# Bias rows on 128 partitions and eight strided loads, a padded weight layout, and attention one step earlier, in a one-layer hybrid of attention and mLSTM

## The chip, the cores and the metric

The kernel runs on one NeuronCore of a Trainium2 chip. A core has five engines with their own instruction streams: TensorE (PE) multiplies matrices, VectorE (DVE), ScalarE (ACT) and GpSimd (POOL) work element by element, and SyncE (SP) issues nearly all DMAs here. Each engine runs its instructions in the order in which they were issued to it, and waits on semaphores for what others produce. The time is that of one execution on the device, in microseconds (us). The profile is of one execution; spans and busy times are from it.

## What is computed

One layer for one sequence of 256 tokens with a model width of 1024. Cut to what matters:

```python
ada = c @ w_ada + b_ada                       # shift, scale, gate
h = rmsnorm(x, norm_w) * (1 + scale) + shift
qa, ka, va, za, qm, km, vm, zm, om, ig, fg, ga, gm = split(h @ w_in)
qa, ka = rmsnorm per head (8 heads of 128)
bias[h, i, j] = rel_bias[bucket(i - j), h]    # 32 buckets; -1e30 where j > i
ya = softmax(qa @ ka.T / sqrt(128) + bias) @ va     # 256 tokens are one block: plain causal attention
ya = (ya * silu(za)) @ w_att_proj
qm, km = silu(causal conv of width 4 over [qm, km])
hm = mLSTM(qm, km, vm, ig, fg)                # 4 heads of 256
ym = (rmsnorm(sigmoid(om) * hm) * silu(zm)) @ w_ml_proj
y = sigmoid(ga) * ya + sigmoid(gm) * ym
out = x + gate * (y @ w_out)
```

All arrays are float32. The bias depends on i - j alone, so a head's bias matrix is made of shifted copies of one row of 384 values: the matrix's row p is that row from place 127 - p on.

## The kernel before

Large products are made from two halves of each operand: a rounded high part (type fp32r) and the rest as a low part, and three products high x high, high x low, low x high. So every weight tile that comes in by DMA (`raw`) is cast by ACT to its high part (`wh`, L448) and then DVE (at eight places POOL) subtracts to get its low part (`wl`, L452).

**Phase 1** (`P1_STEPS`, L303 to L320) makes `hTh` and `hTl`, the modulated input, transposed, in 8 pieces of 128 rows, and at the same time the q and k products (2048 columns of `w_in`, the tensor `w_row`), piece by piece in the order in which their rows come in. A letter of `P1_STEPS` is an operation, its digit the piece. `next_loads` issues the loads of `P1_LOADS`: `A` is half a piece of `w_ada` (512 KB, contiguous), `W` a column range of a piece of `w_row` (`W_PIECES`: 128 rows of 2048 or 6144 bytes). The first row matmul (L198) needs `hTh` of piece 0 (L168) and the cast of `W00` (L183), which stand in ACT's order as `w0`, then `H0`. POOL meanwhile copies the bias table into the row `rvec` (`rel_prep`, L283 to L292). At the end of the phase SP writes it to DRAM (`rel_write`, L301), between loads of `w_va`.

**Phase 2** runs over 23 chunks of at most 512 columns (`chunks`): va in three, then za, qm, km, att, zm, vm, om, ga, gm, ml and out in two halves each. A chunk is four steps g, one for 256 of the 1024 rows that are summed. Steps 0 to 11 are va (12 matmuls of 344 columns a step), 12 to 19 za (24 matmuls of 256 columns), 20 to 35 qm and km. In each step g (loop at L948) the program issues, in this order:

- `split(g + 4)`: ACT's cast, then what `between` hangs on step g, then DVE's low split. So weights are split four steps ahead; a cast waits for its buffer until the matmuls of step g - 1 are done (five buffers).
- at the first step of a chunk, the eviction of the chunk before (`EV`). za's first half is the exception: `ev_za` stands further down, at L969.
- what `at` hangs on step g, in the order of registration
- `pump()`: the next weight loads whose buffer is free (six buffers)
- the step's matmuls

The small work hangs on steps by hand (L867 to L923). `bias_read` at step 0 reads the bias matrices `Tb` (128 rows, 8 heads, 256 columns) back from DRAM in four loads of 32 neighbouring partitions. `qk_T` transposes q and k on PE in two halves of four heads, with an eviction by ACT. Attention of head h runs from `A0`, which is 11: at step A0 + h PE makes the scores (`att_qk`), DVE adds the bias and takes the maximum (L608, L610), ACT the exponential (`att_exp`); a step later DVE normalises (`att_norm`); at A0 + 3 + h PE transposes the probabilities and ACT copies them out (`att_PT`). `att_av` multiplies two heads with va, DVE multiplies with silu(za) (`yf`, L648). `gates_0` to `gates_7`, `gates_T` and `gates_D` make the mLSTM's decay matrices; `gates_2` is a logarithm, `gates_5` and `gates_D` exponentials. ACT loads a table (ACT_TABLE_LOAD) when it changes between these, the attention's exponentials and Silu.

All of this shares four PSUM banks, `aux`, which are given out in turn: the fifth request gets the first bank again and waits until its reader is done. `qk_T` asks for two banks, `att_qk`, `att_PT`, `att_av`, `gates_0` and `gates_T` for one each.

Of the kernel before, what the change touches and what calls it, by code (L numbers as in the profile page):

```python
# [66 lines left out]
def tile_hybrid(ctx: ExitStack, tc: tile.TileContext, x, c, params2, w_row, w_va, ada_mod, ada_gate,  # L67
# [21 lines left out]
    rvec = consts.tile([AH, 384], F32, name="rvec")  # L89
# [9 lines left out]
    rvd = dram.tile([32, AH, 384], F32, name="rvd")  # L99
# [9 lines left out]
    relT = prm[0:AH, P_RT:P_RT + BUCKETS]  # L109
# [173 lines left out]
    def rel_prep(part):  # L283
        bk = rel_bucket_starts()
        one = BUCKETS // 2
        if part == 0:
            nc.gpsimd.tensor_copy(rvec[:, 256 - one:256], relT[:, one:])
        for b in range(one + 4 * part, one + 4 * part + 4):
            ds_ = [d for d in range(S) if bk[d] == b]
            m0, m1 = 255 - max(ds_), 255 - min(ds_) + 1  # L290
            r = BUCKETS - 1 - b
            nc.gpsimd.tensor_copy(rvec[:, m0:m1], relT[:, r:r + 1].to_broadcast([AH, m1 - m0]))  # L292
# [7 lines left out]
    def rel_write():  # L300
        nc.sync.dma_start(rvd.rearrange("b h m -> h b m"), rvec[:, None, :].to_broadcast([AH, 32, 384]))  # L301
# [155 lines left out]
    def at(step, fn, *a):  # L457
        hooks.setdefault(step, []).append((fn, a))
# [38 lines left out]
    def bias_read():  # L497
        L = 384
        Tb = slot("bias", [128, AH, S], F32, "Tb")
        for a in range(4):  # L500
            src = bass.AP(tensor=rvd.tensor, offset=rvd.offset + 127 - 32 * a,
                          ap=[[AH * L - 1, 32], [L, AH], [1, S]])
            nc.sync.dma_start(Tb[32 * a:32 * a + 32], src)
        T["Tb"] = Tb
# [373 lines left out]
    at(5, gates_0)  # L878
    at(6, qk_T, "q", 0)
    at(7, qk_T, "k", 0)  # L880
    at(10, qk_T, "q", 1)
    at(12, qk_T, "k", 1)
    A0 = 11
# [5 lines left out]
    for step, fn in ((6, gates_1), (9, gates_2), (11, gates_3), (13, gates_copy), (14, gates_4), (16, gates_5),  # L889
                     (18, gates_6), (18, gates_T), (19, gates_7), (22, gates_D)):  # L890
        at(step, fn)
# [6 lines left out]
    for q in range(2):  # L898
        at(done("za", 0) + 1 + q, att_av, 2 * q)
        at(done("za", 1) + 1 + q, att_av, 4 + 2 * q)  # L900
# [47 lines left out]
    for g in range(NG):  # L948
# [20 lines left out]
        if g == done("za", 0):  # L969
            ev_za(mmt[C["za", 0]], 0)  # L970
# [55 lines left out]
def _lay_out(x, c, w_ada, b_ada, norm_w, w_in, q_norm_w, k_norm_w, rel_bias, conv_w, conv_b, b_igate, b_fgate,  # L1026
# [6 lines left out]
    params[0:AH, P_RT:] = rel_bias.T[:, ::-1]  # L1033
# [9 lines left out]
    w_row = w_in[0, :, :NR].reshape(KT, 128, NR)  # L1043
# [29 lines left out]
```

## Time and profile before

| | us |
|---|---|
| median of 3 runs (352.56 to 353.26) | 352.77 |
| the profiled execution | 352.9 |
| its span, first to last instruction | 351.1 |
| busy: PE, DVE, ACT, POOL | 345.3, 247.3, 215.8, 89.0 |

The span is 1.8 us shorter than the profiled execution's own time. The granted TensorE clock is 1.000 over the span. A row of a timeline reads: start, duration, engine, line, operation, what it writes <- what it reads, sizes, count, and in brackets how long its engine had been idle before it and what ended that. SPq is SP's queue: the time of a DMA there is that of issuing it. A row of the waits reads: who waited for whom, total us, times, longest.

### The profile page before, as it was taken

Reading aid. Unit: us, or ns where it says so; the run is one execution under the profiler, and the core shown is the slowest. Engines: PE = TensorE matmul, PEld = TensorE weight load, DVE = VectorE, ACT = ScalarE, POOL = GpSimd, SP = SyncE. Lnnn points to the kernel's source line nnn. Section 1 sums busy time; section 2 is a strip of 40 time slices with the busy share of each in tenths; the row PEclk is TensorE's granted clock in tenths of the full one; section 3 lists DMA queues with packets and bytes.
Section 4 is the critical chain, followed back from the end, with each engine's and each line's share of the span. In section 5 each row is a group of like instructions: output and inputs, shape, how many; then the busy total and the mean of one; then the engine's idle time right before and its main releaser. Section 6 shows DMA issues by size and latency. Waiting matters only on the chain.

```text
span 351.1 us, 6176 instructions
## 1 busy us (share of the span) xinstructions
PE 345.3 (98%) x2432; PEld 322.7 (92%) x2432; DVE 247.3 (70%) x369; ACT 215.8 (61%) x333; POOL 89.0 (25%) x81
## 2 busy tenths in 40 slices
PE   8999999999999999999999999999999999999996
PEld 7687889999999999999998888888899999999996
DVE  6899996966976528768975593764475775469961
ACT  4768779978978696775636554545646374443510
POOL 4300002880202443554104252000010420452000
PEclk9999999999999999999999999999999999999999
DMA  7999999996571463393784836649219229382011
GB/s 265 398 414 414 418 417 328 246 257 256 212 271 59 134 227 121 126 410 125 289 311 136 343 121 239 241 148 385 67 23 357 100 53 365 124 269 91 3 62 60
DMA packets 23573, 77.99 MB, mean 222 GB/s; under 512 B 2928, under 2 KB 4984, under 8 KB 22904
## 3 DMA queue, kind: packets, MB, share of 16 engines
q1 hardware_dynamic: 23392, 77.07, 60.9%
q10 hardware_dynamic: 152, 0.53, 0.4%
q8 instruction: 19, 0.31, 0.4%
q14 instruction: 10, 0.08, 0.1%
HBM read 76.14 MB, written 1.45 MB: 221 GB/s over the span
## 4 chain that ended last, share of the span: by engine, by line
PE 82%; DVE 7%; DMA 4%; ACT 4%; issue 1%; POOL 0%; SPq 0%; POOLq 0%; ACTq 0%; DVEq 0%
PE mm L1004 13%; PE mm L1007 13%; PE mm L1006 13%; PE pm L198 12%; PE mm L997 6%; PE mm L998 6%; PE mm L999 6%; DMA raw<-in_w_in_dram 4%; PE mm L990 3%; DVE wl L452 3%; ACT wh L448 2%; PE xps L263 1%; PE mm L1017 1%; PE mm L1019 1%; PE mm L1018 1%
## 5 line engine op out<-in xcount | busy, mean ns | idle before, releaser
L452 DVE TENSOR_TENSOR wl<-raw,wh 128x1024 fp32r<-128x1024 f32 (+1 forms) x92 | 118.9, 1303 | 65.3 <-ACT wh L448 65.3
L448 ACT CAST wh<-raw 128x1024 fp32r<-128x1024 f32 (+1 forms) x100 | 100.6, 1015 | 55.6 <-PE mm L999 25.9
L1004 PE MATMUL mm<-hTh,wh 128*128 128x256 f32 x320 | 90.0, 281 | 0.0
L1007 PE MATMUL mm<-hTh,wl 128*128 128x256 f32 x320 | 88.7, 277 | 0.0
L1006 PE MATMUL mm<-hTl,wh 128*128 128x256 f32 x320 | 88.7, 277 | 0.0
L1006 PEld LDWEIGHTS mm<-hTl,wh 128*128 128x128 f32 x320 | 60.2, 188 | 0.0
L1004 PEld LDWEIGHTS mm<-hTh,wh 128*128 128x128 f32 x320 | 60.2, 188 | 0.0
L1007 PEld LDWEIGHTS mm<-hTh,wl 128*128 128x128 f32 x320 | 60.2, 188 | 0.0
L997 PE MATMUL mm<-wh,hTh 128*128 128x512 f32 (+1 forms) x144 | 53.1, 369 | 0.0
L998 PE MATMUL mm<-wl,hTh 128*128 128x512 f32 (+1 forms) x144 | 52.7, 366 | 0.0
L999 PE MATMUL mm<-wh,hTl 128*128 128x512 f32 (+1 forms) x144 | 52.6, 366 | 0.0
L999 PEld LDWEIGHTS mm<-wh,hTl 128*128 128x128 f32 x144 | 27.0, 188 | 3.8
L997 PEld LDWEIGHTS mm<-wh,hTh 128*128 128x128 f32 x144 | 27.1, 188 | 3.6
L998 PEld LDWEIGHTS mm<-wl,hTh 128*128 128x128 f32 x144 | 27.1, 188 | 3.5
L452 POOL TENSOR_TENSOR wl<-raw,wh 128x1024 fp32r<-128x1024 f32 x8 | 19.5, 2465 | 18.1 <-ACT wh L448 11.8
L183 ACT CAST wrh<-raw 128x512 fp32r<-128x512 f32 (+1 forms) x24 | 18.2, 761 | 9.4 <-DMA raw<-in_w_row_dram 9.3
L188 DVE TENSOR_TENSOR wrl<-raw,wrh 128x512 fp32r<-128x512 f32 (+1 forms) x26 | 20.4, 809 | 2.4 <-ACT wrh L183 2.4
L198 PE MATMUL pm<-wrh,hTh 128*128 128x512 f32 x64 | 20.0, 393 | 0.6 <-ACT hTh L168 0.6
L198 PE MATMUL pm<-wrh,hTl 128*128 128x512 f32 x64 | 19.9, 392 | 0.0
L198 PE MATMUL pm<-wrl,hTh 128*128 128x512 f32 x64 | 19.0, 396 | 0.0
L1007 PE MATMUL mm<-yah,wl 128*128 128x256 f32 x64 | 17.7, 276 | 0.0
L1004 PE MATMUL mm<-yah,wh 128*128 128x256 f32 x64 | 17.7, 276 | 0.0
(218 smaller groups left out, 662.4 us busy)
## 6 DMA issues: line engine op xcount, KB each, us to landing
raw<-in_w_in_dram SPq DMA_DIRECT2D x32, 1024.0 KB, 5.0
adat<-in_ada_mod_dram SPq DMA_DIRECT2D x16, 512.0 KB, 8.7
raw<-in_w_va_dram SPq DMA_DIRECT2D x6, 688.0 KB, 9.5
raw<-in_ada_gate_dram SPq DMA_DIRECT2D x4, 1024.0 KB, 5.9
raw<-in_w_att_proj_dram SPq DMA_DIRECT2D x4, 1024.0 KB, 6.3
raw<-in_w_ml_proj_dram SPq DMA_DIRECT2D x4, 1024.0 KB, 5.9
raw<-in_w_out_dram SPq DMA_DIRECT2D x4, 1024.0 KB, 5.4
raw<-in_w_row_dram SPq DMA_DIRECT2D x15, 256.0 KB, 8.1
```

The source lines that it names most:

```text
L183: copy(wsp[k][0][:, c0:c1], wrow[k][:, c0:c1])
L188: e.tensor_tensor(l[:, cs], wrow[k][:, cs], h[:, cs].bitcast(F32), op=OP.subtract)
L198: nc.tensor.matmul(pm[ch][:, t], a[:, k, t * 128:(t + 1) * 128], b[:, cs], start=k == 0 and i == 0, stop=k == KT - 1 and i == 2)
L448: nc.scalar.copy(h, w)
L452: e.tensor_tensor(l, w, h.bitcast(F32), op=OP.subtract)
L990: nc.tensor.matmul(mmt[ci][:, t, cs], a, w[:, kk, cs], start=first and i == 0 and c0 == 0 and w is wh, stop=last and i == 1 and c0 > 0, sk ...
L997: nc.tensor.matmul(o, a, wh[:, kk], start=first, stop=False)
L998: nc.tensor.matmul(o, a, wl[:, kk], start=False, stop=False)
L999: nc.tensor.matmul(o, b, wh[:, kk], start=False, stop=last)
L1004: nc.tensor.matmul(o, wh[:, kk, cs], sh_[:, k], start=first and i % 2 == 0, stop=False, skip_group_check=True)
L1006: nc.tensor.matmul(o, wh[:, kk, cs], sl_[:, k], start=False, stop=False, skip_group_check=True)
L1007: nc.tensor.matmul(o, wl[:, kk, cs], sh_[:, k], start=False, stop=last and i % 2 == 1, skip_group_check=True)
```

## The change

The bias row is made on all 128 partitions: the host repeats the bias table of the 8 heads 16 times down the partitions, so that partition 8j + h holds head h. It is written to DRAM once per partition (196,608 bytes in all, instead of 32 times from 8 partitions). `bias_read` issues eight loads; load i fills the partitions i, i + 8, ... i + 120, and each of these reads its own copy of the eight rows.

`w_row`, a copy of the first 2048 columns of `w_in` that the host lays out, gets 256 columns of zeros behind each row, which no load reads: rows are 9216 bytes apart instead of 8192.

Attention starts at step 10 instead of 11; the transposes of the first halves of q and k move from steps 6 and 7 to 7 and 8, the gates by one or two steps (`gates_T` by three) to later ones; `att_av` moves from steps 17, 18, 21, 22 to 18, 20, 22, 24; za's first half is evicted in step 17 instead of 16, behind the last exponential of the attention.

```diff
-    rvec = consts.tile([AH, 384], F32, name="rvec")
+    rvec = consts.tile([128, 384], F32, name="rvec")
...
-    rvd = dram.tile([32, AH, 384], F32, name="rvd")
+    rvd = dram.tile([128, 384], F32, name="rvd")
...
-    relT = prm[0:AH, P_RT:P_RT + BUCKETS]
+    relT = prm[:, P_RT:P_RT + BUCKETS]
...
-            nc.gpsimd.tensor_copy(rvec[:, m0:m1], relT[:, r:r + 1].to_broadcast([AH, m1 - m0]))
+            nc.gpsimd.tensor_copy(rvec[:, m0:m1], relT[:, r:r + 1].to_broadcast([128, m1 - m0]))
...
-        nc.sync.dma_start(rvd.rearrange("b h m -> h b m"), rvec[:, None, :].to_broadcast([AH, 32, 384]))
+        nc.sync.dma_start(rvd, rvec)
...
-        for a in range(4):
-            src = bass.AP(tensor=rvd.tensor, offset=rvd.offset + 127 - 32 * a,
-                          ap=[[AH * L - 1, 32], [L, AH], [1, S]])
-            nc.sync.dma_start(Tb[32 * a:32 * a + 32], src)
+        for i in range(8):
+            src = bass.AP(tensor=rvd.tensor, offset=rvd.offset + 127 - i,
+                          ap=[[AH * L - 8, 16], [L, AH], [1, S]])
+            nc.sync.dma_start(Tb[i:128:8], src)
...
-    at(5, gates_0)
-    at(6, qk_T, "q", 0)
-    at(7, qk_T, "k", 0)
+    at(7, qk_T, "q", 0)
+    at(7, gates_0)
+    at(8, qk_T, "k", 0)
+    at(8, gates_1)
     at(10, qk_T, "q", 1)
+    at(10, gates_2)
     at(12, qk_T, "k", 1)
-    A0 = 11
+    A0 = 10
...
-    for step, fn in ((6, gates_1), (9, gates_2), (11, gates_3), (13, gates_copy), (14, gates_4), (16, gates_5),
-                     (18, gates_6), (18, gates_T), (19, gates_7), (22, gates_D)):
+    for step, fn in ((12, gates_3), (14, gates_copy), (15, gates_4), (17, gates_5), (19, gates_6), (20, gates_7),
+                     (21, gates_T), (23, gates_D)):
...
-        at(done("za", 0) + 1 + q, att_av, 2 * q)
-        at(done("za", 1) + 1 + q, att_av, 4 + 2 * q)
+        at(done("za", 0) + 2 + 2 * q, att_av, 2 * q)
+        at(done("za", 1) + 2 + 2 * q, att_av, 4 + 2 * q)
...
-        if g == done("za", 0):
+        if g == A0 + AH - 1:
             ev_za(mmt[C["za", 0]], 0)
...
-    params[0:AH, P_RT:] = rel_bias.T[:, ::-1]
+    params[:, P_RT:] = np.tile(rel_bias.T[:, ::-1], (16, 1))
...
-    w_row = w_in[0, :, :NR].reshape(KT, 128, NR)
+    w_row = np.zeros((KT, 128, NR + 256), w_in.dtype)
+    w_row[:, :, :NR] = w_in[0, :, :NR].reshape(KT, 128, NR)
```

## The prediction

> **What bounds the kernel now.** I read the share of each engine first, then the groups of instructions (count, busy us and mean ns of one, idle time before them and what ended it), then the windows, then the order of time around the places that the change touches.
>
> ```profile
> PE 345.3 (98%) x2432; PEld 322.7 (92%) x2432; DVE 247.3 (70%) x369; ACT 215.8 (61%) x333; POOL 89.0 (25%) x81
> ```
>
> ```profile
> L198 PE MATMUL pm<-wrh,hTh 128*128 128x512 f32 x64 | 20.0, 393 | 0.6 <-ACT hTh L168 0.6
> L642 PE MATMUL aux<-PT,vat 128*128 128x256 f32 x16 | 4.9, 386 | 0.4 <-DVE yf L648 0.4
> ```
>
> ```profile
> 26.30:35.00 8.70, 8.66 (x38) 6.66 (x37) 8.42 (x14) 7.12 (x13) 0.00 (x0) 1.00 1.03 413
> 52.70:61.40 8.70, 8.70 (x51) 8.08 (x50) 5.41 (x8) 8.70 (x12) 2.41 (x2) 1.00 0.99 328
> 61.40:70.00 8.60, 8.60 (x61) 8.51 (x60) 8.60 (x10) 7.79 (x13) 7.58 (x6) 1.00 1.06 246
> 70.00:79.00 9.00, 9.00 (x64) 8.97 (x64) 6.11 (x6) 6.88 (x10) 7.83 (x6) 1.00 1.05 258
> ```
>
> TensorE is busy for 345.3 us, 98% of the span, and in the windows (length, then busy PE, PEld, DVE, ACT, POOL, granted clock, DMA share, GB/s) it fills the stretches of the change at a granted clock of 1.00. So the change can take off only what TensorE waits, 351.1 - 345.3 = 5.8 us in all, and can add wherever it makes TensorE wait. Two of its waits lie where the change reaches: 0.6 us at the first row matmul and 0.4 us at the products of probabilities and values. The chain of waits runs through DVE, ACT and a w_in load up to that second wait, at 107.95 us, and through TensorE behind it; what is saved before that wait, and not in it, is not saved in time. The DMA engines are full from 52.7 to 79 us (share 0.99 to 1.06) but move 328, 246 and 258 GB/s where the same share moved 413 before: this is the stretch of the bias traffic.
>
> **The change, part by part.** *Attention one step earlier, za's eviction and the products later.*
>
> ```profile
> 102.78 1.28 ACT L663 ACT_TABLE_LOAD   x1
> 104.08 1.03 ACT L663 ACTIVATE zat<-mm 128x1024 f32<-128x1024 f32 x1
> 105.00 1.04 ACT L448 CAST wh<-raw 128x1024 fp32r<-128x1024 f32 x1
> 106.07 1.22 DVE L452 TENSOR_TENSOR wl<-raw,wh 128x1024 fp32r<-128x1024 f32 x1 [2.59 <-ACT wh L448]
> 107.22 0.68 DVE L648 TENSOR_TENSOR yf<-aux,zat 128x512 f32<-128x512 f32 x1
> 107.95 0.48 PE L642 MATMUL aux<-PT,vat 128*128 128x256 f32 x1 [0.43 <-DVE yf L648]
> ```
>
> The four aux banks go round. Step 18 before takes four of them (att_PT of head 4, att_qk of head 7, gates_T, att_av of heads 2 and 3), so its att_av gets the bank that step 17's att_av has just filled, and waits until DVE has read it (yf). DVE is late because ACT loads a table (1.28) and evicts za (1.03) ahead of the cast of step 21's weights. After the change att_av comes at steps 18, 20, 22 and 24, gates_T at 21, and a step takes two or three banks: the second att_av reuses a bank that an ACT copy freed a step earlier, and the first one's bank is asked for again only by gates_T, three steps later. The wait of 0.43 us goes, and with it the restart after it: the matmul behind it takes 0.48 where its group's mean is 0.386, so 0.1 more. **Term: -0.5 us.** za is evicted after the last exponential instead of among them, so two table loads (1.28 each) leave ACT; ACT is 61% busy, and TensorE has no wait on it there but the one counted, so I cost them at nothing. Holding za's first accumulator a step longer costs nothing either: mm has two banks, and the next to need this one is step 20.
>
> *Bias rows on 128 partitions.* The copies that make rvec run on POOL, with as many instructions of the same row length, so the same. What changes is traffic.
>
> ```profile
> 46.38 0.34 SPq L301 DMA_DIRECT2D rvd<-rvec  x1
> 59.68 2.85 SPq L503 DMA_DIRECT2D Tb<-rvd  x4
> ```
>
> ```profile
> SPq L503 <- DMA rvd<-rvec: 1.3, 1, 1.3
> ```
>
> ```profile
> DMA to landing us min/median/max: 14.9/15.6/16.4
> ```
>
> The write goes from 384 KB out of 8 partitions to 192 KB out of 128; the reads stay at 1 MB in rows of 1 KB. SP issues eight instead of four: 2.85 us for four, so about as much again, less the 1.3 us that SP waited for the write and that a smaller write should free; the w_in load behind them (step 14's weights) is issued up to 1.5 us later or not at all later. Against 413 GB/s the three windows fall short by (413-328)/413 x 8.7 = 1.8, (413-246)/413 x 8.6 = 3.5 and (413-258)/413 x 9.0 = 3.4 us. I give the first to the write, and the other 6.9 us to the reads and what shares the engines with them. So step 14's load, which landed at about 80.4 (ACT's cast below), lands between 80.4 - 1.8 - 0.5 (half the write's bytes) = 78.1 with reads as slow as now and 71.2 with reads at the full rate; if the write gains nothing and the issues cost, 80.4 to 81.9. [...] I take 77. For TensorE this is worth nothing by itself, since it does not wait there; it is the cover that the earlier attention needs.
>
> [...]
>
> *Rows of w_in 9216 bytes apart.*
>
> ```profile
> 7.00:9.00 2.00, 2.00 (x19) 2.00 (x19) 1.96 (x3) 0.40 (x1) 2.00 (x4) 1.00 0.86 200
> 9.00:11.00 2.00, 1.62 (x15) 1.43 (x13) 0.88 (x3) 0.88 (x2) 2.00 (x12) 1.00 0.97 377
> 13.00:15.00 2.00, 2.00 (x10) 1.55 (x10) 1.84 (x4) 2.00 (x4) 0.00 (x0) 1.00 1.05 413
> ```
>
> ```profile
> 8.78 1.84 PE L263 MATMUL xps<-diag,xt 128*128 128x128 f32 x15
> 10.12 0.62 ACT L183 CAST wrh<-raw 128x512 fp32r<-128x512 f32 x1 [2.42 <-DMA raw<-in_w_row_dram]
> 10.64 0.56 ACT L168 ACTIVATE hTh<-xps,Bb,Ab 128x256 fp32r<-128x256 f32 x1
> 11.26 0.74 PE L198 MATMUL pm<-wrh,hTh 128*128 128x512 f32 x2 [0.64 <-ACT hTh L168]
> ```
>
> While the very first piece (128 rows of 2 KB, 8 KB apart) is read, at 7 to 9.5 us, the engines move 200 GB/s. ACT waits 2.42 us for it, its hTh comes after that cast, and the first row matmul waits 0.64 us for hTh. The shortfall is (413-200)/413 x 2 + (413-377)/413 x 2 = 1.2 us. But pieces of the same size and the same pitch are read at 13 to 15 us with 413 GB/s, and all the later ones too (413 at 26 to 35). If the pitch were to blame they should be slow. I take 0, with ends of -1.2 (the piece lands 1.2 us earlier and TensorE follows, from 0.64 us of wait and the low splits behind it) and +0.3: DMA and TensorE are both full from 26 to 35 us (share 1.03; 8.66 of 8.70 busy), so a lower rate there would show, but 9216 bytes leaves rows as long as they were.
>
> **Sum:** -0.5 + 0 + 0. The profiled execution took 352.9 us (span 351.1, 1.8 around it), so 352.4; it stands 0.13 above the median of the runs, 352.77, so **352.3 us**.
>
> **The rivals.**
>
> *The pitch was to blame.* For it: the first piece alone is at half rate at a pitch of a power of two. Against it: its followers. It gives -0.5 - 1.0, between the wait of 0.64 and the shortfall of 1.2: 351.3 us. [...]
>
> *TensorE waits at att_qk of head 3 (slower).* Moved to step 10, attention's chain starts behind ACT's cast of step 14's weights, and the new order of aux banks makes att_qk of head 3, at step 13, reuse the bank of head 2, which DVE frees in step 12, one step before instead of two.
>
> ```profile
> 76.22 1.28 ACT L539 ACT_TABLE_LOAD   x1
> 77.52 0.41 ACT L539 ACTIVATE G<-G 4x256 f32<-4x256 f32 x1
> 80.38 1.05 ACT L448 CAST wh<-raw 128x1024 fp32r<-128x1024 f32 x1 [2.44 <-DMA raw<-in_w_in_dram]
> 81.33 1.26 ACT L494 ACTIVATE qT<-aux,qns 128x512 f32<-128x512 f32 x2
> 83.89 1.28 ACT L616 ACT_TABLE_LOAD   x1
> 85.18 0.51 ACT L616 ACTIVATE P<-P,st 128x256 f32<-128x256 f32 x1
> 86.08 1.03 ACT L448 CAST wh<-raw 128x1024 fp32r<-128x1024 f32 x1
> ```
>
> ```profile
> 90.39 0.15 DVE L622 RECIPROCAL st<-st 128x2 f32<-128x2 f32 x1
> 91.04 0.41 DVE L608 CUSTOM_DVE_ANT_0 P<-aux,Tb 128x256 f32<-128x256 f32 x1
> 91.59 1.22 DVE L452 TENSOR_TENSOR wl<-raw,wh 128x1024 fp32r<-128x1024 f32 x1
> ```
>
> ```profile
> 76.85 1.04 PE L492 MATMUL aux<-ident,qt 128*128 128x128 f32 x8
> 82.16 0.59 PE L604 MATMUL aux<-kT,qT 128*128 128x256 f32 x2
> 82.81 1.04 PE L492 MATMUL aux<-ident,kt 128*128 128x128 f32 x8
> 86.51 0.60 PE L604 MATMUL aux<-kT,qT 128*128 128x256 f32 x2
> 89.91 0.27 PE L629 MATMUL aux<-ident,P 128*128 128x128 f32 x1
> 90.23 0.60 PE L604 MATMUL aux<-kT,qT 128*128 128x256 f32 x2
> ```
>
> If that cast starts at X, ACT does in order: cast 0.95 (80.38 to 81.33), two evictions 1.26, table and Ln 1.7 (76.22 to 77.93), table 1.29, exponential of head 0 0.9 (85.18 to 86.08): X + 6.1. Then DVE and ACT by turns: norm 0.65 (90.39 to 91.04), head 1's bias and minimum 0.55 (91.04 to 91.59), exponential 0.9, 0.3 more for the low split that DVE still holds, norm 0.65, head 2's 0.55: X + 9.7. TensorE asks for the bank at 86.51 (step 13 before) + 0.6 (one att_qk more ahead of it, 82.16 to 82.81) + 0.3 (three transposes, 89.91 to 90.23) = 87.4. TensorE frees the cast's buffer when it starts step 10, at 76.85, so X is at least 77.0, and the bank is free at 86.7: no wait. It decides from X = 77.7: each microsecond of a later landing is a microsecond of wait. Against it: 77 is likely. For it: the margin is 0.7. With the landing as before (80.4) the wait is 2.7, the time 352.3 + 2.7 = **355.0 us**.
>
> *The bias reads gain nothing.* With the landing at 78.1 the wait is 0.4, and eats most of the 0.5: 352.7 us. [...]
>
> **How the numbers follow.** Forecast (352.3) 0.40; pitch (351.3) 0.33; wait at head 3 with a landing past 79 (353.4 to 355) 0.12; reads gain nothing (352.7) 0.15. The range takes in forecast, pitch and the fourth case, and the beginning of the third: 350.9 to 353.4; the forecast's own is 351.8 to 352.7. A measurement of this kernel tells about 0.2% from no change (0.7 us): under 352.07 lie most of the pitch case (0.30) and a part of the forecast (0.10); above 353.48 most of the third case (0.10): faster 0.40, same 0.50, slower 0.10.
>
> **What would show it.** Right: no wait of L642 on yf; one table load for Silu and one for the exponentials up to step 20; SP no longer waiting for the write; ACT's cast of step 14's weights waiting for TensorE and not for DMA. The pitch: 7 to 9 us at about 400 GB/s and the first row matmul near 10.6 instead of 11.26. Wrong: a wait of TensorE on DVE's P (L608 or L610) around 87 us, or the same 200 GB/s at the start together with a gain of over 1 us.

## The result, and the profile after

The changed kernel takes 356.56 us (median of six runs, 355.62 to 357.31) against 352.82 us for the kernel before in the same comparison: a ratio of 1.0097 (95% interval 1.0069 to 1.0124). It is slower by 3.7 us, where 352.3 us had been predicted, with a range of 350.9 to 353.4. The profiled execution took 357.09 us, with a span of 355.2 us. Two slow runs are left out of the ratios of this document, one of the kernel before at 897.61 us and one of the run e18_fill, below, at 390.2 us.

Line numbers behind the new bias loads and schedule are two higher than before from the main matmuls on: L997, L998, L1004, L1006 and L1007 are now L999, L1000, L1006, L1008 and L1009. The conv lines (L676, L682, L687) and the lines of attention keep their numbers.

The page of the changed kernel, the busy time of each engine and the group of matmuls with the largest wait (count, busy us and mean ns of one, idle time before them and what ended it):

```profile
PE 346.5 (98%) x2432; PEld 325.6 (92%) x2432; DVE 245.9 (69%) x369; ACT 213.5 (60%) x331; POOL 90.8 (26%) x81
...
L1006 PE MATMUL mm<-hTh,wh 128*128 128x256 f32 x320 | 91.2, 285 | 2.3 <-DVE qmT L682 2.3
```

TensorE is busy for 1.2 us more with the same 2432 matmuls, and there is one long wait in the middle that the kernel before does not have: 2.3 us on DVE's conv (L682). The two waits that the change could remove, of L198 and of L642, are gone. At the start, the x transposes (L263) wait 1.7 us for ACT instead of 0.2; that wait differs from profile to profile in this case (0.2 us in e2, 1.2 us in e11), and the changed kernel is ahead behind it all the same.

Where the 4.1 us of span came from is read by laying the same instructions of both traces side by side. First the kernel before (timeline of TensorE: start, length; then two lines' first and last start):

```profile
56.20 0.32 PE L997 MATMUL mm<-wh,hTh 128*128 128x344 f32 x1
140.52 0.28 PE L1004 MATMUL mm<-hTh,wh 128*128 128x256 f32 x1
```

```profile
L762 PE MATMUL aux<-qms,kms x24: 281/283/364, 192.6 to 213.1; 128*128 128x256 f32 x24
```

```profile
L816 PE MATMUL aux<-ident,omt x16: 270/272/273, 266.8 to 282.4; 128*128 128x128 f32 x16
```

And the changed kernel, the same views:

```profile
55.12 0.32 PE L999 MATMUL mm<-wh,hTh 128*128 128x344 f32 x1
141.38 0.55 PE L1006 MATMUL mm<-hTh,wh 128*128 128x256 f32 x1 [2.27 <-DVE qmT L682]
```

```profile
L762 PE MATMUL aux<-qms,kms x24: 281/283/364, 195.0 to 215.5; 128*128 128x256 f32 x24
```

```profile
L816 PE MATMUL aux<-ident,omt x16: 270/272/273, 269.2 to 284.6; 128*128 128x128 f32 x16
```

| place | before | after | after behind by |
|---|---|---|---|
| step 0 of the second phase | 56.20 | 55.12 | -1.1 |
| first matmul of step 28 | 140.52 | 141.38 | +0.9 |
| first mLSTM scores (L762) | 192.6 | 195.0 | +2.4 |
| last ml_T (L816) | 282.4 | 284.6 | +2.2 |
| end of the span | 351.1 | 355.2 | +4.1 |

So the changed kernel is ahead by 1.1 us at step 0, and by 1.4 just before step 28 (141.38 - 2.27 = 139.11 against 140.52). Then it loses three times: 2.3 us in the wait at step 28, 1.5 us between there and the scores, and 1.9 us behind the last ml_T.

*The wait.* The timeline of the changed kernel on ACT and DVE around conv of qm's first half:

```profile
125.22 1.28 ACT L595 ACT_TABLE_LOAD   x1
...
129.00 0.39 ACT L596 ACTIVATE NM<-NM,gc 128x128 f32<-128x128 f32 x1
129.29 1.04 ACT L448 CAST wh<-raw 128x1024 fp32r<-128x1024 f32 x1
130.24 1.00 ACT L676 ACTIVATE qmT<-mm,prm 128x256 f32<-128x256 f32 x2
...
131.28 2.43 DVE L682 SCALAR_TENSOR_TENSOR qmT<-mm,prm,qmT 128x255 f32<-128x255 f32 x6 [8.28 <-ACT qmT L676]
133.62 0.69 DVE L648 TENSOR_TENSOR yf<-aux,zat 128x512 f32<-128x512 f32 x1
134.34 0.62 ACT L649 CAST yah<-yf 128x512 fp32r<-128x512 f32 x1 [3.10 <-DVE yf L648]
...
137.76 1.01 ACT L676 ACTIVATE qmT<-mm,prm 128x256 f32<-128x256 f32 x2
...
138.80 2.43 DVE L682 SCALAR_TENSOR_TENSOR qmT<-mm,prm,qmT 128x255 f32<-128x255 f32 x6 [1.37 <-ACT qmT L676]
```

Conv works in two parts, each an ACT eviction (L676) and six DVE operations (L682) on the accumulator of qm's first half, and step 28 needs that accumulator's bank. Here gates_D (L595 and L596), now at step 23, holds ACT from 125.22 to 129.29; behind the first eviction ACT then stands still for 3.10 us, because the cast of yah for heads 6 and 7 (att_av, now at step 24) waits for yf, which DVE makes only behind the first conv part. The second part ends at 138.80 + 2.43 = 141.23, and TensorE starts at 141.38. Before, the second part ended at 137.15 + 2.44 = 139.59, and step 28 began at 140.52 without a wait:

```profile
137.15 2.44 DVE L682 SCALAR_TENSOR_TENSOR qmT<-mm,prm,qmT 128x255 f32<-128x255 f32 x6 [1.20 <-ACT qmT L676]
```

*Right behind the wait.* Two windows of the changed kernel (length, busy PE, PEld, DVE, ACT, POOL with counts, granted clock, DMA share, GB/s):

```profile
138.00:141.00 3.00, 1.10 (x10) 0.91 (x8) 2.20 (x6) 1.70 (x3) 0.00 (x0) 1.00 0.00 0
141.20:144.40 3.20, 3.02 (x14) 3.06 (x15) 1.16 (x2) 3.08 (x5) 1.43 (x1) 0.50 0.44 164
```

After the pause TensorE runs at a granted clock of 0.50 for these 3.2 us and does 14 matmuls where 3.2 us hold 28 at 113 ns. That is the second loss.

*Behind the last ml_T.* The same window, first of the kernel before, then of the changed kernel:

```profile
290.00:320.00 30.00, 30.00 (x267) 30.00 (x266) 18.82 (x13) 12.37 (x12) 11.36 (x4) 1.00 0.66 244
```

```profile
290.00:320.00 30.00, 30.00 (x257) 30.00 (x256) 17.35 (x13) 14.54 (x15) 10.70 (x5) 1.00 0.69 249
```

TensorE is full in both, at the same granted clock, but starts 267 matmuls in one and 257 in the other. The starts lie 113 ns apart before and 118 ns after, from the last ml_T until 331.7 us. That is the third loss, about 1.8 of the 1.9 us.

*What went as meant.* The start and the bias stretch of the changed kernel, by windows:

```profile
7.00:9.00 2.00, 1.45 (x13) 1.45 (x14) 1.76 (x3) 0.80 (x2) 2.00 (x5) 1.00 1.03 415
9.00:11.00 2.00, 2.00 (x20) 2.00 (x19) 1.91 (x4) 1.35 (x3) 2.00 (x7) 1.00 1.01 419
```

```profile
52.70:61.40 8.70, 8.70 (x53) 8.27 (x52) 6.40 (x8) 8.70 (x12) 2.90 (x3) 1.00 1.02 419
61.40:70.00 8.60, 8.60 (x61) 8.56 (x60) 8.60 (x10) 6.07 (x10) 8.18 (x6) 1.00 0.89 230
70.00:79.00 9.00, 9.00 (x64) 8.93 (x63) 6.42 (x10) 8.79 (x14) 4.33 (x5) 1.00 0.92 360
```

The first piece of w_in comes at 415 GB/s instead of 200, the stretch from 52.7 us at 419 instead of 328. The bias loads go out from 55.1 to 65.1 us (59.7 before):

```profile
L503 SPq DMA_DIRECT2D Tb<-rvd x8: 532/589/636, 55.1 to 65.1; - x8
...
DMA to landing us min/median/max: 2.8/8.9/9.8
```

The last has landed by 67.8 us, before by 77.0.

### The profile page after: what moved, and what is told of

Read it like the earlier page. It is cut to its first block, busy times and chain, and to the rows that moved or that the text cites. A ratio compares the mean times of both kernels' runs of the same rounds, so it can differ in the third digit from the quotient of the medians.

```text
span 355.2 us, 6174 instructions
## 1 busy us (share of the span) xinstructions
PE 346.5 (98%) x2432; PEld 325.6 (92%) x2432; DVE 245.9 (69%) x369; ACT 213.5 (60%) x331; POOL 90.8 (26%) x81
## 4 chain that ended last, share of the span: by engine, by line
PE 93%; ACT 2%; DVE 2%; DMA 1%; issue 0%; POOL 0%; DVEq 0%; ACTq 0%; POOLq 0%
PE mm L1006 14%; PE mm L1008 14%; PE mm L1009 14%; PE pm L198 12%; PE mm L999 8%; PE mm L1000 8%; PE mm L1001 8%; PE mm L992 3%; DVE qmT L682 1%; PE xps L263 1%; DMA xt<-in_x_dram 1%; PE mm L1021 1%; PE mm L1020 1%; PE mm L1019 1%; PE aux L492 1%; PE aux L604 1%
## 5 line engine op out<-in xcount | busy, mean ns | idle before, releaser
L452 DVE TENSOR_TENSOR wl<-raw,wh 128x1024 fp32r<-128x1024 f32 (+1 forms) x92 | 117.6, 1289 | 65.7 <-ACT wh L448 65.7
L1006 PE MATMUL mm<-hTh,wh 128*128 128x256 f32 x320 | 91.2, 285 | 2.3 <-DVE qmT L682 2.3
L1008 PE MATMUL mm<-hTl,wh 128*128 128x256 f32 x320 | 89.7, 280 | 0.0
L1009 PE MATMUL mm<-hTh,wl 128*128 128x256 f32 x320 | 89.6, 280 | 0.0
L1006 PEld LDWEIGHTS mm<-hTh,wh 128*128 128x128 f32 x320 | 61.2, 191 | 2.5 <-issue 2.4
L1008 PEld LDWEIGHTS mm<-hTl,wh 128*128 128x128 f32 x320 | 60.9, 190 | 0.0
L1009 PEld LDWEIGHTS mm<-hTh,wl 128*128 128x128 f32 x320 | 60.8, 190 | 0.0
L999 PE MATMUL mm<-wh,hTh 128*128 128x512 f32 (+1 forms) x144 | 53.0, 368 | 0.0
L1000 PE MATMUL mm<-wl,hTh 128*128 128x512 f32 (+1 forms) x144 | 52.6, 365 | 0.0
L999 PEld LDWEIGHTS mm<-wh,hTh 128*128 128x128 f32 x144 | 27.1, 188 | 3.6
L1000 PEld LDWEIGHTS mm<-wl,hTh 128*128 128x128 f32 x144 | 27.1, 188 | 3.5
L452 POOL TENSOR_TENSOR wl<-raw,wh 128x1024 fp32r<-128x1024 f32 x8 | 19.5, 2458 | 21.9 <-ACT wh L448 14.9
L198 PE MATMUL pm<-wrh,hTh 128*128 128x512 f32 x64 | 19.9, 391 | 0.0
L198 PE MATMUL pm<-wrh,hTl 128*128 128x512 f32 x64 | 19.7, 389 | 0.0
L198 PE MATMUL pm<-wrl,hTh 128*128 128x512 f32 x64 | 18.7, 391 | 0.0
L682 DVE SCALAR_TENSOR_TENSOR qmT<-mm,prm,qmT 128x255 f32<-128x255 f32 (+2 forms) x24 | 9.7, 475 | 12.2 <-ACT qmT L676 12.1
L1006 PE MATMUL mm<-ymh,wh 128*128 128x256 f32 x64 | 18.0, 281 | 0.0
```

The costliest lines, as they stand in the source:

```text
L198: nc.tensor.matmul(pm[ch][:, t], a[:, k, t * 128:(t + 1) * 128], b[:, cs], start=k == 0 and i == 0, stop=k == KT - 1 and i == 2)
L452: e.tensor_tensor(l, w, h.bitcast(F32), op=OP.subtract)
L682: nc.vector.scalar_tensor_tensor(d, pt[:, i, :S - sh], col(P_CW + 16 * j + base + i), d, op0=OP.mult, op1=OP.add)
L999: nc.tensor.matmul(o, a, wh[:, kk], start=first, stop=False)
L1000: nc.tensor.matmul(o, a, wl[:, kk], start=False, stop=False)
L1006: nc.tensor.matmul(o, wh[:, kk, cs], sh_[:, k], start=first and i % 2 == 0, stop=False, skip_group_check=True)
```

## The experiments

Each is the named kernel with the edit that is shown or told. Ratios are against runs of the kernel before on the same chip (medians of 352.8 to 353.5 us there). A trace is of one run of each kernel.

### What makes the wait at step 28

Two theories had each one move as the cause, a third the mere earliness of TensorE. **e1_av23** moves the last att_av back by one step:

```diff
-        at(done("za", 1) + 2 + 2 * q, att_av, 4 + 2 * q)
+        at(done("za", 1) + 2 + 1 * q, att_av, 4 + 2 * q)
```

> The changed kernel with one hook moved: the last att_av (heads 6 and 7) at step 23 instead of 24, ahead of gates_D and of conv(qm, 0, 0) in program order. Changed kernel: TensorE waits 2.4 us at 138.8 for the mm bank that conv(qm, 0, 1) on DVE still holds, the clock record falls to 0.5 for 3.4 us right behind it, and the kernel takes 356.6 us. Theory A: ACT's cast of yah (heads 6 and 7) waits 3.1 us for yf, which stands behind conv on DVE, and holds up the conv silu and evict behind it; the move takes the wait of the cast to under 0.5 us, the TensorE wait to 0.6 us or less, no half clock: 352.5 to 353.5 us where the matmuls behind ml_T run at 118 ns, 351 to 352 where they run at 113 ns. Rival B (gates_D one step later holds ACT up): the wait of TensorE stays at 1.5 us or more, about 355 to 357 us. Rival C (TensorE only arrives 1.6 us earlier at a conv that ends when it ended before): the wait stays at 1 us or more and conv(qm, 0, 1) ends near 139.5 us as in the kernel before.

354.96 us, ratio 1.0063 (1.0041 to 1.0086). Its page has the wait at

```profile
L1006 PE MATMUL mm<-hTh,wh 128*128 128x256 f32 x320 | 90.8, 284 | 0.6 <-DVE qmT L682 0.6
```

No half clock follows that wait (the granted clock is 1.00 from 139.5 to 143 us). The time is above the 352.5 to 353.5 us of theory A all the same: in this profile the matmuls from step 28 to about 184 us come every 118 ns instead of 113, which is told below.

**e2_gd22** moves gates_D back and leaves att_av late:

```diff
-                     (21, gates_T), (23, gates_D)):
+                     (21, gates_T), (22, gates_D)):
```

> The changed kernel with gates_D at step 22 instead of 23, as in the kernel before, and the last att_av left at step 24. Theory A: the cast of yah still waits for yf behind conv on DVE, some 2 to 3 us, and TensorE still waits 1.5 us or more at step 28; 354.5 to 357 us. Rival B (gates_D is what makes ACT late): wait at step 28 of 0.6 us or less, 351 to 353.5 us. Rival C: wait at 1 us or more in this run and in the run with att_av at step 23 alike.

353.90 us, ratio 1.0023 (1.0004 to 1.0042). No wait is left at step 28, although ACT waits for yf as long as in the changed kernel:

```profile
128.14 1.02 ACT L676 ACTIVATE qmT<-mm,prm 128x256 f32<-128x256 f32 x2
129.19 2.43 DVE L682 SCALAR_TENSOR_TENSOR qmT<-mm,prm,qmT 128x255 f32<-128x255 f32 x6 [5.86 <-ACT qmT L676]
131.53 0.68 DVE L648 TENSOR_TENSOR yf<-aux,zat 128x512 f32<-128x512 f32 x1
132.25 0.62 ACT L649 CAST yah<-yf 128x512 fp32r<-128x512 f32 x1 [3.10 <-DVE yf L648]
...
135.67 1.00 ACT L676 ACTIVATE qmT<-mm,prm 128x256 f32<-128x256 f32 x2
136.71 2.43 DVE L682 SCALAR_TENSOR_TENSOR qmT<-mm,prm,qmT 128x255 f32<-128x255 f32 x6 [1.37 <-ACT qmT L676]
...
139.28 0.36 PE L1006 MATMUL mm<-hTh,wh 128*128 128x256 f32 x1
```

Conv ends at 136.71 + 2.43 = 139.14 and step 28 starts 0.14 us behind it, as close as in the changed kernel (141.23 and 141.38): the late att_av alone uses up the whole slack, but no more.

Neither theory held as it stood: the one that blamed att_av alone wanted a wait of 1.5 us here, the one that blamed gates_D alone a wait of 1.5 us in e1_av23. Both moves delay the second conv part: its eviction comes at 137.76 in the changed kernel, at 136.05 without the late att_av (1.7 us earlier), at 135.67 without the late gates_D (2.1 us earlier).

**e8_both** makes both moves:

> The changed kernel with gates_D at step 22 and the last att_av at step 23. Theory A (and B): no wait over 0.3 us at step 28, no half clock behind it. Both losses gone, 2.4 and 1.5 us: 352.6 us where the matmuls behind ml_T run at 118 ns as in the profiled run of the changed kernel, 351.1 us where they run at 113 ns as in the kernel before. Rival C: a wait of 1 us or more stays, 354 us or more.

353.11 us, ratio 1.0002 (0.9992 to 1.0013).

```profile
134.57 1.00 ACT L676 ACTIVATE qmT<-mm,prm 128x256 f32<-128x256 f32 x2
...
135.61 2.43 DVE L682 SCALAR_TENSOR_TENSOR qmT<-mm,prm,qmT 128x255 f32<-128x255 f32 x6 [1.28 <-ACT qmT L676]
```

The eviction is 3.2 us earlier than in the changed kernel, and conv ends at 138.04, 0.9 us ahead of step 28 (138.98), the same slack as in the kernel before. There is no wait and no half clock, and TensorE is 1.54 us ahead of the kernel before from step 28 to 264 us; then the pace behind ml_T takes all of it back. (With that pace 352.6 us had been expected.)

**e15_gates_only** and **e16_att_only** keep pad and bias rows and make only the moves of the gates, or only those of attention and att_av. Of the lines that the change added, each keeps, among others:

```diff
 e15: attention and att_av at the old steps
+                     (21, gates_T), (23, gates_D)):
...
 e16: gates at the old steps
+    A0 = 10
...
+        at(done("za", 1) + 2 + 2 * q, att_av, 4 + 2 * q)
```

> Pad and bias rows as in the changed kernel, gates on their new steps (gates_D at 23), attention and att_av on their old ones (last att_av at 22). The casts of yah are then all ahead of gates_D. Theory 'both moves together': gates_D puts ACT back by some 2 us, the cast of yah no longer stands behind conv, so a wait of 0.3 to 1.2 us at step 28 as in the run e1_av23, no half clock; 352 to 353 us if the matmuls behind the last ml_T run at 113 ns, 353.5 to 354.5 us if at 118 ns, which would put the slow pace on the moved gates.

> Pad and bias rows as in the changed kernel, attention one step earlier and att_av at 18, 20, 22 and 24, gates on their old steps (gates_D at 22). Theory 'both moves together': as in the run e2_gd22, ACT waits about 3 us for yf of heads 6 and 7 but no wait over 0.3 us reaches TensorE at step 28; 351.3 to 351.8 us if the matmuls behind the last ml_T run at 113 ns, 353 us if at 118 ns, which would put the slow pace on the moved attention.

e15 takes 352.74 us, ratio 1.0004 (0.9981 to 1.0027), e16 351.91 us, ratio 0.9963 (0.9945 to 0.9981). The gates alone bring a wait, larger than expected; e16 has none. The row is of e15:

```profile
140.26 0.36 PE L1006 MATMUL mm<-hTh,wh 128*128 128x256 f32 x1 [1.46 <-DVE qmT L682]
```

So with gates_D at 23 there is a wait of 0.6 to 2.3 us (e1, e15, e4, the changed kernel), with gates_D at 22 there is none, wherever att_av stands (e2, e8, e16). **gates_D is what the wait needs; the late att_av adds 1.6 us to it** (2.27 against 0.64 in e1), because it has used up the slack.

**e4_sched_only** is the kernel before with the whole new schedule, old bias rows and old pitch:

> The kernel before with the schedule of the changed kernel (attention from step 10, gates and att_av moved) and its old bias rows and old pitch. Prediction's rival: the w_in load of step 14 lands behind the bias at about 80 us, and TensorE waits 2 to 3 us at att_qk of head 3. Then TensorE arrives at step 28 later, and the wait for conv there is between 0 and 1.5 us. Theory A: the cast of yah waits for yf as in the changed kernel, and conv(qm, 0, 1) ends at 141 us or later; 354.5 to 357 us. Rival C: no wait at step 28 once TensorE is not 1.6 us early, and 352.3 to 355.5 us.

363.71 us, ratio 1.029 (1.0229 to 1.0352), the slowest of all. TensorE stops twice in attention and again at step 28:

```profile
80.44 1.05 ACT L448 CAST wh<-raw 128x1024 fp32r<-128x1024 f32 x1 [3.14 <-DMA raw<-in_w_in_dram]
```

```profile
88.07 0.33 PE L629 MATMUL aux<-ident,P 128*128 128x128 f32 x1 [0.65 <-DVE st L610]
...
90.42 0.70 PE L604 MATMUL aux<-kT,qT 128*128 128x256 f32 x2 [1.80 <-DVE st L610]
```

```profile
145.52 0.36 PE L1006 MATMUL mm<-hTh,wh 128*128 128x256 f32 x1 [2.27 <-DVE qmT L682]
```

TensorE comes to step 28 about 4 us later than in the changed kernel and still waits 2.27 us, and in e8 it comes as early (138.98) and does not wait: the third theory, that it only came too early, is out. The first two waits belong to the prediction's rival, told below. The profiled run, at 359.57 us, is the fastest of four, and above everything that had been expected (352.3 to 357). The others took 363.22 to 364.96 us, at mean clocks of 0.991 to 0.995; what they lost is not shown.

### What the pad and the bias rows are worth

**e3_pad_only** is the kernel before with the pad:

```diff
-    w_row = w_in[0, :, :NR].reshape(KT, 128, NR)
+    w_row = np.zeros((KT, 128, NR + 256), w_in.dtype)
+    w_row[:, :, :NR] = w_in[0, :, :NR].reshape(KT, 128, NR)
```

> The kernel before with rows of w_in 9216 bytes apart instead of 8192 and nothing else. The prediction took the pad for 0 with ends -1.2 and +0.3. Theory 'pitch was to blame': the stretch from 7 to 9 us moves about 415 GB/s instead of 200, step 0 of the second phase begins about 1.1 us earlier, 351.7 us. Rival 'start-up noise or the smaller bias write made the gain': 7 to 9 us stays near 200 GB/s and the time at 352.8. A wait of TensorE at att_qk of head 3 or att_av may eat up to 0.5 of the gain, as attention keeps its steps and the bias its late landing.

351.90 us, ratio 0.9973 (0.9961 to 0.9985). **e7_pitch16k** is the changed kernel with `2 * NR` for `NR + 256`:

> The changed kernel with rows of w_in 16384 bytes apart instead of 9216. If a pitch of a power of two is what halves the rate of the first w_in load: 200 GB/s or less from 7 to 9 us again, ACT waits 2.4 us or more for its first piece, and step 0 of the second phase begins 1 us or more later than in the changed kernel. TensorE then arrives later at step 28 and waits about 1 us less there, so the time may stay at 355 to 357.5 us. If something else than the pitch's power of two did it (any pad): 415 GB/s.

358.09 us, ratio 1.0159 (1.0133 to 1.0184). The windows from 7 to 9 us of e3 and of e7:

```profile
7.00:9.00 2.00, 1.87 (x16) 1.87 (x17) 1.00 (x3) 0.48 (x2) 1.92 (x7) 1.00 1.03 376
```

```profile
7.00:9.00 2.00, 2.00 (x19) 2.00 (x20) 1.91 (x3) 0.40 (x1) 2.00 (x4) 1.00 1.04 311
```

The pad is worth about 0.9 us. From 7 to 9 us the engines move 376 to 431 GB/s in the fourteen profiles with 9216 bytes, and 200 to 245 in the four with 8192; step 0 of the second phase begins between 55.04 and 55.86 us in the former, and between 55.94 and 56.42 in the latter. At 16384 bytes the rate is 311 GB/s, between the two, where 200 or less had been expected, or 415; step 0 begins at 55.50, among those of 9216. So it is the pitch of 8192 that slows the first piece, and not every power of two does so as much; why is not settled. The median of e7 lies above the 355 to 357.5 us that were expected. Its profile (357.62 us) follows that of the changed kernel, 0.4 to 0.6 us behind from step 0 to the end; what its slower runs lost is not shown.

**e5_bias_only** is the kernel before with the bias rows alone (rvec and rvd on 128 partitions, eight reads):

> The kernel before with the bias rows made on 128 partitions, one write of 196 KB and eight reads, and with the old schedule and pitch. If the bias rows are worth nothing by themselves: SP no longer waits for the write, Tb lands at 66 to 68 us instead of 74.6 to 77, ACT's cast of step 14 no longer waits for its load, and no wait of TensorE goes or comes: 352.4 to 353.2 us. Rival 'the smaller write frees the DMA queues near 50 to 60 us and is the source of the 1.1 us by which the changed kernel is ahead at step 0': 351.7 us.

352.82 us, ratio 0.9989 (0.9979 to 0.9999). The wait of att_av at 107 us is gone, with the old schedule:

```profile
105.54 0.68 DVE L648 TENSOR_TENSOR yf<-aux,zat 128x512 f32<-128x512 f32 x1
...
107.18 0.70 PE L642 MATMUL aux<-PT,vat 128*128 128x256 f32 x2
```

DVE makes yf at 105.54 instead of 107.22, and TensorE asks for the bank at 107.18 and has it. The expectation that no wait would go was wrong: with the load of step 14's weights no longer late, ACT makes head 0's exponentials at 82.15 instead of 85.18 and za at 102.41 instead of 104.08, and DVE its yf as much earlier.

**e6_neigh** is the changed kernel with eight reads of 16 neighbouring partitions each:

```diff
-                          ap=[[AH * L - 8, 16], [L, AH], [1, S]])
-            nc.sync.dma_start(Tb[i:128:8], src)
+                          ap=[[AH * L - 1, 16], [L, AH], [1, S]])
+            nc.sync.dma_start(Tb[16 * i:16 * i + 16], src)
```

> The changed kernel with each of its eight bias reads filling 16 neighbouring partitions instead of every eighth partition; bytes, write and issue are the same. If the spread over partitions is what made the reads faster (median 8.9 us in the changed kernel): each read takes 11 to 15 us, Tb lands 3 to 6 us later, near 71 to 74 us. If the smaller size of one read and the missing wait of SP did it: landing within 1.5 us of the changed kernel's 65.6 to 67.8. The time in both cases is that of the changed kernel, 355.6 to 357.3 us, unless the w_in load of step 14 gets late enough for TensorE to wait at att_qk of head 3.

356.42 us, ratio 1.0104 (1.0081 to 1.0127).

```profile
L503 SPq DMA_DIRECT2D Tb<-rvd x8: 302/418/430, 55.1 to 66.5; - x8
...
DMA to landing us min/median/max: 3.4/11.1/11.6
```

The median read takes 11.1 us instead of 8.9, and the last lands at 70.0 instead of 67.8 us. This lies between the two expectations. The spread over partitions is worth 2 us of the 9 by which the bias came earlier, and nothing of the time.

**e9_old_sched** keeps pad and bias rows and has the old schedule:

> The changed kernel with the schedule of the kernel before: bias rows on 128 partitions and rows 9216 bytes apart stay, attention, gates and att_av go back to their old steps. If the schedule alone brought the loss, and the gains of the pad (ratio 0.9973 by itself) and of the bias rows (0.9989 by itself) add: no wait at step 28, the wait of att_av at 107 us back at 0.3 to 0.7 us, the matmuls behind the last ml_T at 113 ns, 351.5 us. If pad or bias rows have a part in the loss (TensorE early by 1 us): a wait over 0.5 us at step 28 and 352.8 us or more.

351.56 us, ratio 0.9964 (0.9952 to 0.9977). The two gains add, and **this beats both kernels**. The wait of att_av did not come back, as had been expected of it: its matmuls (L642) have no wait here either. The whole loss, 5.0 us against the changed kernel's 356.56, is the schedule's. **e20_att_av23** is e16 with the last att_av at 23:

> The kernel of the run e16_att_only (pad, bias rows, attention one step earlier, gates on their old steps; 351.91 us) with the last att_av at 23 instead of 24, which should take away ACT's wait of 3 us for yf. Nothing at step 28 waits in either, so no time follows from that: 351.3 to 351.9 us where the 256-column matmuls run at 113 ns, 1.5 us more in runs where a stretch of them runs at 118 ns. It is to show whether attention one step earlier beats the old steps (e9_old_sched, 351.56 us): theory 'once the bias rows land early the wait of att_av is gone anyway': no, within 0.3 us of it.

351.76 us, ratio 0.9951 (0.9929 to 0.9973): level with e9 and e16. Attention one step earlier, done without its two side effects, brings nothing that the early bias rows have not brought already.

### The half clock

**e18_fill** and **e19_fill10** put matmuls of `ident`, 20 and 10 of them, ahead of step 28 in the changed kernel:

```diff
+    def fill():
+        pa = aux([128, 2, 256])
+        for _ in range(10):
+            nc.tensor.matmul(pa[:, 0, 0:128], ident, ident, start=True, stop=True)
+
+    at(done("qm", 1), fill)
```

> The changed kernel with 20 matmuls of 128 columns (about 2.2 us) ahead of step 28, on a spare aux bank, so that TensorE works through most of the wait for conv; the wait itself stays. The changed kernel's runs fall in two groups, 355.6 to 356.0 us (clock 0.998 to 1.0) and 357.1 to 357.3 us (clock 0.994 to 0.995). Theory 'the idle 2.4 us is what sets off the half clock': every run at 355.4 to 356.1 us, clock 0.998 or more. Rival 'the half clock comes from something else at that place': again two groups, some runs at 357 us or more.

> The changed kernel with 10 matmuls ahead of step 28, on a spare aux bank: in the run e18_fill each took two passes of about 110 ns, 4.4 us in all, so that step 28 began 1.9 us late and nothing of the wait was left; ten should fill 2.2 us of the 2.4. The changed kernel's runs and those of e6_neigh, with the same wait, fell in two groups: 355.6 to 356.0 us (clock 0.998 to 1.0) and 357.1 to 357.7 us (clock 0.994 to 0.995). Theory 'idleness of 2.4 us sets off the half clock': every run at 355.4 to 356.2 us, none at a clock under 0.997. Rival 'it comes from something else there': again some runs at 357 us or more with a clock of 0.995.

e18: 359.32 us, ratio 1.0176 (1.0151 to 1.0202); the filling put step 28 1.9 us later (143.32 against 141.38), and in its profile the matmuls come every 118 ns from there to about 187 us; 355.4 to 356.1 had been expected. e19: 356.57 us, ratio 1.0088 (1.0061 to 1.0116). Its filling and the window that stood at a clock of 0.50:

```profile
139.68 2.39 PE L906 MATMUL aux<-ident 128*128 128x128 f32 x20
142.11 0.36 PE L1012 MATMUL mm<-hTh,wh 128*128 128x256 f32 x1
```

```profile
141.20:144.40 3.20, 3.17 (x28) 3.00 (x28) 1.90 (x3) 2.34 (x3) 0.69 (x1) 1.00 0.39 124
```

Of the 14 runs with the idle wait of 2.3 us at step 28 and no other such stop (changed kernel, e6, e7) eight have a mean clock of 0.995 or less, which is what 3.4 us at half clock come to (1.7 of 355 us); the 0.50 itself is seen in the two of them that were profiled, of the changed kernel and of e7. With the pause filled, all six runs of e19 and four of e18 have 1.0. The idleness sets off the half clock, in about half of the runs. It is not the only thing that lowers the mean clock: so do 3 of the 102 runs of the kernels whose profile has no wait over 0.7 us there (one each of e5, e10 and e20), and one of ten of e15, whose wait is 1.46 us.

What it costs is seen in e6, whose profiled run has the same wait, starts step 28 at the same time and keeps its clock:

```profile
141.38 0.36 PE L1006 MATMUL mm<-hTh,wh 128*128 128x256 f32 x1 [2.26 <-DVE qmT L682]
```

```profile
141.20:144.40 3.20, 3.02 (x26) 3.05 (x27) 1.17 (x2) 3.08 (x5) 1.43 (x1) 1.00 0.43 164
```

Its last ml_T starts at 283.1 us, the changed kernel's at 284.6: 1.5 us.

The time of e19 is not the 355.4 to 356.2 that was expected for every run (355.44 to 357.23), and its median is no lower than the changed kernel's: the filling took the half clock away, but no gain shows in the medians. In its profile (356.39) step 0 began 0.7 us later than in the changed kernel's, and step 28 as well (142.11 against 141.38), so the filling itself put nothing back, and at the last ml_T it is 0.7 us ahead (283.9 against 284.6). The other five runs have no profile, and what spreads them is not shown.

### The slow pace behind ml_T

**e10_pe2**, **e11_pe1** and **e12_before_pe1** shift all later instructions of TensorE: by two places and by one in e8_both, and by one in the kernel before:

```diff
 e10: WARM = 6 instead of 5
 e11, e12: ahead of the first x transpose
+            nc.tensor.matmul(pw[:, 0, 0:128], xt[:, 0, 0:128], ident, start=True, stop=True)
```

> The kernel of the run e8_both (gates_D at 22, last att_av at 23) with one warm-up matmul more ahead of the first x transposes, which puts every later instruction of TensorE two places on (3325 instead of 3323 before the first ml_T; the kernel before has 3324). In e8_both the 256-column matmuls behind the last ml_T came every 118 ns until 328 us, in the kernel before every 113 ns. Theory P (the pace follows the place in TensorE's instruction stream): the pace may change, and if it goes by odd and even places it stays 118 ns, 353.1 us. Theory T (the new order of the other engines makes it): 118 ns, 353.1 us.

> The kernel of the run e8_both with a matmul on x, written to the warm-up bank, ahead of the first x transpose. It takes over one of the two waits of that transpose, so that every later instruction of TensorE stands one place on (3324 before the first ml_T, as in the kernel before). Theory P: 113 ns behind the last ml_T, 351.5 to 351.8 us. Theory T: 118 ns, 353.1 to 353.4 us.

> The kernel before with the same matmul on x ahead of the first x transpose, and nothing else: every later instruction of TensorE stands one place on (3325 before the first ml_T, the count of e10_pe2). Theory P: the pace in some stretch changes, and with it the time, by up to 1.5 us (if by odd and even: 118 ns behind the last ml_T, 354.3 us). Theory T: paces as in the kernel before, 352.8 to 353.1 us.

353.12, 353.02 and 353.43 us (ratios 1.0010, 1.0003 and 1.0017 with intervals of 0.9992 to 1.0028, 0.9992 to 1.0014 and 1.0001 to 1.0033). In the profiles e10 and e11 keep 118 ns behind the last ml_T and e12 keeps 113: a shift by one or two places in the instruction stream does not change it. In the window from 290 to 320 us, e9 and then e8:

```profile
290.00:320.00 30.00, 30.00 (x267) 30.00 (x266) 18.86 (x14) 12.46 (x13) 11.00 (x4) 1.00 0.64 229
```

```profile
290.00:320.00 30.00, 30.00 (x257) 30.00 (x257) 19.24 (x12) 11.74 (x12) 11.22 (x4) 1.00 0.57 226
```

All eleven profiles that move both the gates and attention have the slow pace in that stretch; none of the eight others has, those with one of the two moves (e15, e16, e20) among them. So, as far as one profile of each kernel can tell, it goes with the schedule as a whole, though nothing of that schedule runs after 150 us. In e16's profile, as in those of e1 and e18, another stretch, 139 to 184 us, ran at 118 ns, and cost it the 1.7 us by which that run (353.58) stands above its median; the times of e16 fall in two groups (eight at 351.7 to 352.1, two at 353.5 to 353.6), so it may come in some runs and not in others, which no trace shows. What the two paces hang on stays open.

## Why the prediction was wrong

**Attention moved, -0.5 us.** The wait of L642 on yf did go. But it goes with the bias rows alone (e5, e9), so the move was worth nothing beside them; the prediction gave the move a gain and the bias rows none. That the wait was gone in the changed kernel confirms nothing of this term.

**"so two table loads (1.28 each) leave ACT; ... so I cost them at nothing."** This is the step that failed: the sum has -0.5 us for the whole new schedule, with nothing for ACT and no term for the moved gates, and on top of pad and bias rows the schedule measured +5.0 us (e9 at 351.56, the changed kernel at 356.56). The prediction followed the moved hooks through attention and asked what ACT saves; the two table loads did leave. It did not ask what gates_D at step 23 and att_av at step 24 are put in front of: conv of qm at steps 24 and 25, on ACT and DVE, with an accumulator that step 28 needs. The slack was there to be read, 0.9 us between the end of conv (137.15 + 2.44) and step 28 at 140.52. gates_D holds ACT for 4 us and came one step nearer to conv; the cast of yah moved behind conv's six DVE operations of 2.43 us. Price: 2.3 us of wait, and behind it the half clock and the slow pace, below. The signs that the prediction named for being right came, no wait of L642, one table load each for Silu and the exponentials, no wait of SP for the write, and the time was wrong: they all lay where it had looked.

**What a wait costs beyond itself.** The prediction added 0.1 us for the restart after a wait. Here the restart cost 1.5 us in about half of the runs, through the half clock (e6 beside the changed kernel; gone with the pause filled, e18 and e19).

**Bias rows, worth nothing, landing at 77.** SP's wait for the write went, as foreseen, and ACT's cast of step 14's weights no longer waits for its load. The reads began 4.6 us earlier (55.1 against 59.7) and took 12.7 us from the first issue to the last landing (67.8) instead of 17.3 (77.0). One reading was wrong: SP took 10.49 us for the eight issues, not twice 2.85, because twice, for 5.6 us in all, it waited there for a w_in load, so the load of step 14's weights went out at 65.72 instead of 62.63, 3.1 us later and not 1.5 at most. Its weights were cast by 76.95 even so, where ACT before began that cast at 80.38; the rival that the reads gain nothing did not come. The worth was 0.3 us by time (0.9989), not 0, and hardly clear of it.

Reads as slow as before, on which the later end of 78.1 stood, did not come: the same 1 MB took 12.7 us instead of 17.3, and 14.9 with 16 neighbours to a read (e6, 55.1 to 70.0), at a median of 11.1 us a read instead of 8.9. Why the choice of partitions matters was not shown.

**The pad, taken for 0.** It was worth 0.9 us, nearly its end of -1.2. The argument against it, that later pieces of the same pitch come at 413 GB/s, was true and did not decide: only the first piece is slow (200 GB/s from 7 to 9 us), and at 9216 bytes it is not (415); at 16384 it is less slow (311, e7). The rival "the pitch was to blame" was the right one. Its sign, a first row matmul near 10.6 us, came in some profiles (10.41 in e1, 10.55 in e8) and not in that of the changed kernel (11.14): the start scatters by more than the gain, which is read at step 0.

**The slower rival, a wait at att_qk of head 3.** Its mechanism was right and it did not decide. With the old bias rows (e4) ACT's cast starts at 80.44, the prediction's worked case, and TensorE waits 0.65 + 1.80 = 2.45 us for DVE, where 2.7 had been worked out; the 1.80 stands at att_qk, as foreseen, the 0.65 at the transposes of the probabilities just ahead of it. In the changed kernel the early bias covers it.

**Two more terms that the prediction did not have** are larger than those that it had: the half clock, 1.5 us, and the slow pace, 1.8 us. The second could not have been worked out from the trace of before, and its cause is not known now.

## What to carry to other kernels

When a hook is moved by one step, ask of every engine that it uses what stands directly behind it in that queue, and which accumulator or buffer waits for that; here the work moved out of attention's way landed in front of conv. Of several edits made together, time each alone and each left out: the two small ones gained 1.2 us, and the large one lost 5.0 on top of them and 10.9 without them. A wait that appears on TensorE may cost more than its length (here 1.5 us behind one of 2.3, in about half of the runs), so a short one is worth avoiding; that filling it pays is not shown here.

## What the hardware showed unexpectedly

An idle gap of 2.3 us on TensorE was followed by a granted clock of 0.50 for about 3.4 us in 8 of 14 runs (seen in two profiles, read from the mean clock in the other six), and in none of the ten runs with the gap filled that the ratios take in (e18, e19). In the profile of the changed kernel the clock was back at 1.00 by 144.6 us, where the gap had ended at 141.38.

Matmuls of 256 columns start 113 or 118 ns apart at the same granted clock of 1.00, in stretches of a few to nearly 50 us. In the profiles that were read for it the pace changes at a block of small matmuls, at another kind of matmul, or at the first matmul of step 28 where TensorE has just stopped or come level with conv (e1, e16). From the last ml_T to 331.7 us the difference is 1.8 us.
